# Attention products in float32, the two heads of a pair by turns, in four mixers of a three-block network

## The chip, the cores and the metric

One core of a Trainium2 chip runs the whole network as one program. The metric is the device time of one execution in microseconds; lower is better. All inputs and outputs are float32.

## The reference

The network takes 256 tokens of width 1024 through three blocks, with 16 heads of 64 (8 in the last mixer). Each mixer ends in the same sum: probabilities times values, head by head.

```python
def reference(x, ...):
    x = first_block(x, ...)    # FoX attention, then NSA attention, RMS norms
    x = second_block(x, ...)   # 8 stick-breaking + 8 dilated-window heads, then SwiGLU
    return third_block(x, ...) # pool mixer + MoBA attention (8 heads), then PEER experts

# fox_mixer, per block of 128 queries
logits = einsum('bhqd,bhkd->bhqk', q, k) * scale + c_q - c_k     # causal mask
p = softmax(logits)
outs.append(einsum('bhqk,bkhd->bqhd', p, v))
return (o * silu(z)) @ w_out

# nsa_mixer: 3 branches per head, gated
o = g0 * (p_c @ v_c) + g1 * (p_s @ v_s) + g2 * (p_w @ v_w)       # compressed, selected, window
return (o * silu(z)) @ w_out
```

With 256 tokens all selected blocks and windows cover the whole causal past, so each branch but the compressed one is 256 x 256 causal attention: a query block of 128 has 128 or 256 keys, three blocks of 128 x 128 in all.

## The kernel before, in words

Activations lie transposed, width on the 128 partitions and the 256 tokens along the free axis. A big projection (`proj`, `mm3`, lines 456 to 460) is done in F32R, a rounded float32 that TensorE streams faster: input and weight are each split into a high and a low part, and each tile takes three products, high x high, low x high, high x low. The weights come by DMA (SP's queue) as 128 x 1024 tiles, ScalarE makes the high part (line 241), VectorE the low part (line 242), some tiles ahead.

Inside a mixer the attention is woven between projections. `weave(main, (side, rate))` runs the generator of the projections, and after each step lets the side generator take some steps at the rate given (0.4 in fox, 4 in NSA, 0.55 in mixer2, 0.4 in mixer3). That sets the order in which the code is emitted; a scheduler then sets each engine's own order from it, which is fixed when the program is built. PE, ScalarE (ACT), VectorE (DVE) and GpSimd (POOL) each take their instructions in that order.

In each mixer a head pair is one 128-row tile (`c`): head 2c in rows 0 to 63, head 2c+1 in rows 64 to 127. For a head the scores are made (line 553), normalised to `pn` [128, 384] (line 586), transposed by PE in three 128 x 128 pieces (lines 592 to 594, or `transposed`, line 624), and copied from PSUM. The 384 columns are 256 queries for the first 128 keys and 128 queries for the second. Then come the AV products, of which there are two forms:

- Fox and mixer2 use F32R. `values` (lines 609 and 610) splits the values into `vh` and `vl` when the projection is read out of PSUM; `probs` (lines 618 and 619) splits the probabilities of a head pair into `pth` (ACT) and `ptl` (DVE); `pair_av` (line 636) makes 6 products for the pair, with the values of both heads as 128 stationary columns and the probabilities of both heads streaming, three of 512 columns and three of 256. Only one half of the result's rows is of use for each head, so `o` is [128, 2, 256], and `gated_pair` (line 654, fox) or `finish` (line 1131, mixer2) reads it in two halves. In mixer2's stick-breaking heads the probabilities come as `ptw` straight out of an exponential on ACT (line 1178), not by a transpose.
- NSA and mixer3 use float32. `attn_transpose` copies the transposed probabilities to `ptw` (line 596, DVE or ACT); `attn_av` makes two products for one head, 256 and 128 query columns (lines 603 and 604), with 64 stationary columns `vN`.

In NSA a side step makes two branches of two heads, and the compressed branch `comp` (lines 982 to 1001), a chain of one PE, eight DVE and one ACT instruction. Then `trans` transposes four probability tiles and, last, the compressed ones (line 1012), and `av` puts the compressed product (line 1021) and the four heads' products into one `o`. In mixer3 the AV product of a head comes two steps behind its scores.

The stretches of the trace are: fox 0 to 163 us (woven from 44 to 134), NSA 163 to 357 (206 to 331), mixer2 357 to 500 (375 to 476), SwiGLU to 703, mixer3 703 to 870 (735 to 820), PEER to the end.

Of the kernel before, what the change touches and what calls it, by code (L numbers as in the profile page):

```python
# [9 lines left out]
F32 = mybir.dt.float32  # L10
# [5 lines left out]
OP = mybir.AluOpType  # L16
# [254 lines left out]
def program(tc, A, out, upto=99):  # L271
    nc = tc.nc
    ctx = ExitStack()
    with ctx:
# [325 lines left out]

        def attn_av(o, pt, v, start=True, stop=True):

            nc.tensor.matmul(o, v(0), pt[:, 0:256], start=start, stop=False)
            nc.tensor.matmul(o[:, 128:256], v(1), pt[:, 256:384], start=False, stop=stop)

        def values(dst, c, p, r):

            hi, lo = (t[:, c[0], c[1]] for t in dst)
            nc.scalar.mul(hi, p, r)
            nc.vector.scalar_tensor_tensor(lo, p, r, hi.bitcast(F32), op0=OP.mult, op1=OP.subtract)  # L610

        def probs(pt, h, src):


            if h % 2 == 0:
                pt[h // 2] = [ph.tile([P, 2, 384], F32R, name=n, bufs=2) for n in ("pth", "ptl")]
            hi, lo = (t[:, h % 2, :] for t in pt[h // 2])
            nc.scalar.copy(hi, src)
            nc.vector.tensor_tensor(lo, src, hi.bitcast(F32), op=OP.subtract)

        def transposed(pn):
            p = ps.tile([P, 384], F32, name="t")
            for i in range(3):
                nc.tensor.transpose(p[:, i * P:i * P + P], pn[:, i * P:i * P + P], ident)
            return p

        def pair_av(pt, v, c):


            o = ps.tile([P, 2, S], F32, name="o")  # L630
            hi, lo = pt
            for kb in range(2):
                q = slice(0, S) if kb == 0 else slice(S, S + P)
                vh, vl = (t[:, kb, c] for t in v)
                for i, (w, x) in enumerate(((vh, hi), (vl, hi), (vh, lo))):
                    nc.tensor.matmul(o[:, :, kb * P:], w, x[:, :, q], start=kb == 0 and i == 0, stop=kb == 1 and i == 2)
            return o

# [7 lines left out]
        def gated(og, c, po, sz):  # L646
            t = wk.tile([P, S], F32, name="sp")
            nc.vector.tensor_tensor(t, po, sz[:, c, :], op=OP.mult)
            split(og, c, t)

        def gated_pair(og, c, o, sz):
            t = wk.tile([P, S], F32, name="sp")
            for e, a in enumerate(HALF):
                nc.vector.tensor_tensor(t[a], o[a, e, :], sz[a, c, :], op=OP.mult)
            split(og, c, t)
# [32 lines left out]
        def fox(st1):  # L688
# [50 lines left out]

            vN = [ph.tile([P, 2, D], F32R, name=n) for n in ("vh", "vl")]  # L740

            def v_evac(c, tb, p):
                if held:
                    f_evac(*held.pop())
                values(vN, (tb, slice(c * 512, c * 512 + 512)), p, rc[:, tb:tb + 1])

# [10 lines left out]
            def fox_attn():  # L757
                st, pt = {}, {}
                for i in range(NH + 3):
                    if i < NH:  # L760
                        h = i
                        while cnt["qk"] <= h // 2:
                            yield
                        pe, s = attn_scores((sel[:, h:h + 1].to_broadcast([P, P]), c3), C["causal"], stacks[h // 2], h % 2)
                        st[h] = attn_norm(pe, s)
                        yield
                    if 1 <= i <= NH:
                        probs(pt, i - 1, transposed(st[i - 1]))
                        yield
                    if i >= 3 and i % 2 == 1:  # L770
                        c = (i - 3) // 2
                        o = pair_av(pt.pop(c), vN, slice(c * P, c * P + P))
                        while cnt["z"] <= c:
                            yield
                        gated_pair(og, c, o, sz)
                        yield
# [17 lines left out]
        def nsa(st1):  # L794
# [159 lines left out]
            def attn():  # L954
# [48 lines left out]

                def trans(c):
                    for e in range(2):
                        for b in range(2):
                            stage[c, e, b] = attn_transpose(stage[c, e, b], CP[b])
                            yield
                    p = ps.tile([32, 256], F32, name="t")
                    c2 = stage[c, "c"]  # L1010
# [4 lines left out]
                    stage[c, "c"] = t  # L1015
                    yield

                def av(c):
                    gp = c // 4
                    o = ps.tile([P, S], F32, name="o")  # L1020
                    nc.tensor.matmul(o, VCB[:, gp, :], stage[c, "c"], start=True, stop=False)
                    for e in range(2):
                        oh = o[e * 64:e * 64 + 64, :]
                        g = 2 * gp + e
                        for b in range(2):
                            attn_av(oh, stage[c, e, b], lambda kb: vN[:, kb, b * 256 + g * 64:b * 256 + g * 64 + 64], False, b == 1)
                            yield
                    while cnt["z"] <= c:
                        yield
                    gated(og, c, o, sz)  # L1030
                    yield

                for i in range(9):
                    if i:
                        while len(done) < 2:
                            yield
                        yield from comp(i - 1)
                    if i < 8:
                        while cnt.get("nq", 0) <= i:
                            yield  # L1040
                        yield from scores(i)
                    if i:
                        yield from trans(i - 1)
                        yield from av(i - 1)

# [47 lines left out]
        def mixer2(st1):  # L1093
# [18 lines left out]

            vN = [ph.tile([P, 2, D], F32R, name=n) for n in ("vh", "vl")]

            def v_evac(c, tb, p):
                values(vN, (tb, slice(c * 512, c * 512 + 512)), p, rc[:, tb:tb + 1])

# [10 lines left out]
            def finish(c, po):  # L1128
                o = ph.tile([P, S], F32, name="fo", bufs=2)
                for e, a in enumerate(HALF):  # L1130
                    nc.scalar.copy(o[a], po[a, e, :])
                sq = wk.tile([P, S], F32, name="sq")
                nc.scalar.activation(sq, o, AF.Square)
                p = ps.tile([P, S], F32, name="t")
# [8 lines left out]
            def attn():  # L1143
                st, pt = {}, {}

                for i in range(19):
# [36 lines left out]
                    if i >= 3 and i % 2 == 1 and i <= 17:  # L1183
                        c = (i - 3) // 2
                        finish(c, pair_av(pt.pop(c), vN, slice(c * P, c * P + P)))
                        yield
# [73 lines left out]
        def mixer3(st1):  # L1260
# [58 lines left out]
            def attn():  # L1319
                st, po = {}, {}  # L1320
                for i in range(11):
# [8 lines left out]
                    if 1 <= i <= 8:  # L1330
                        st[i - 1] = attn_transpose(st[i - 1])
                        yield
                    if 2 <= i <= 9:
                        h = i - 2
                        c = h // 2
                        if h % 2 == 0:
                            po[c] = ps.tile([P, S], F32, name="o")
                        attn_av(po[c][(h % 2) * 64:(h % 2) * 64 + 64, :], st[h], lambda kb: vN[:, kb, h * 64:h * 64 + 64])
                        if h % 2 == 1:
                            nc.scalar.copy(oa[0][:, c, :], po[c])  # L1340
                            nc.vector.tensor_tensor(oa[1][:, c, :], po[c], oa[0][:, c, :].bitcast(F32), op=OP.subtract)
                        yield
# [415 lines left out]
```

## Time and profile before

| what | value |
|---|---|
| median of 3 runs | 1694.55 us (1691.9 to 1695.58) |
| the profiled execution | 1694.25 us |
| its span in the trace | 1692.4 us |
| mean granted TensorE clock | 0.994 |
| PE, DVE, ACT, POOL busy | 96%, 77%, 58%, 11% |
| woven part of fox, NSA, mixer2, mixer3 | 90, 125, 101, 85 us |

A row of the timeline gives the start, the duration, the engine, the line, the operation, its output and inputs, the sizes, and in brackets the idle time before it with the instruction that ended it. Matmuls overlap, so the price of one is the distance between two starts, not its duration. The mean durations of groups and the waits are sums over the window named.

### The profile page before, as it was taken

The page shows a single profiled execution, that of the slowest core. Times are in us where ns is not written, and L with a number is a line of the kernel's source. Part 1 is how long each engine was busy: PE and PEld are TensorE (multiplying, and loading weights), DVE is VectorE, ACT ScalarE, POOL GpSimd, SP SyncE. Part 2 cuts the span into 40 slices and gives each one's busy share as a digit, 9 for nine tenths or more (in the row PEclk, how much of TensorE's full clock was granted, in tenths as well). Part 3 has the DMA queues.
Part 4 walks back from the last instruction along what each step waited for, and adds up shares of the span by engine and source line. Part 5 has one row for each costly group of instructions (what it writes and reads, how often), then busy time and mean ns, then how long its engine had stood idle before and what let it go on. Part 6 is the DMA issues. An engine that isn't in the chain of part 4 may idle for free. (4 is left out here: it accounts for less than half of the span.)

```text
span 1692.4 us, 31723 instructions
## 1 busy us (share of the span) xinstructions
PE 1628.3 (96%) x12052; PEld 1500.7 (89%) x12052; DVE 1301.9 (77%) x2715; ACT 976.2 (58%) x1853; POOL 189.4 (11%) x198
## 2 busy tenths in 40 slices
PE   8999899989899999999999999999999999999997
PEld 7999888778789999889989899999999988888886
DVE  7888788689866776777668998889999656666665
ACT  6875567558855455566644555555544555555554
POOL 2000244340130000111037000000000000000000
PEclk9999999999999999999999999999999999999999
DMA  7445551277537787545545445555455556555563
GB/s 256 138 138 155 163 174 63 103 262 239 173 101 245 256 267 242 165 128 166 187 153 174 162 162 175 163 164 163 164 171 162 187 189 197 193 193 193 193 195 116
DMA packets 84088, 300.07 MB, mean 177 GB/s; under 512 B 10144, under 2 KB 11040, under 8 KB 83680
## 3 DMA queue, kind: packets, MB, share of 16 engines
q1 hardware_dynamic: 83360, 296.39, 53.4%
q8 instruction: 94, 1.54, 0.4%
q10 hardware_dynamic: 576, 1.66, 0.3%
q14 instruction: 58, 0.48, 0.1%
HBM read 296.04 MB, written 1.05 MB: 176 GB/s over the span
## 5 line engine op out<-in xcount | busy, mean ns | idle before, releaser
L242 DVE TENSOR_TENSOR wlo<-wraw,whi 128x1024 fp32r<-128x1024 f32 x486 | 600.6, 1239 | 160.5 <-ACT whi L241 158.0
L241 ACT CAST whi<-wraw 128x1024 fp32r<-128x1024 f32 x504 | 529.9, 1054 | 330.4 <-PE pj L459 104.1
L458 PE MATMUL pj<-hxh,whi 128*128 128x256 f32 x1448 | 411.9, 285 | 7.7 <-DVE vl L610 5.2
L460 PE MATMUL pj<-hxh,wlo 128*128 128x256 f32 x1448 | 405.1, 280 | 1.7 <-DVE wlo L242 1.1
L459 PE MATMUL pj<-hxl,whi 128*128 128x256 f32 x1448 | 405.5, 280 | 0.7 <-DVE hxl L1201 0.4
L458 PEld LDWEIGHTS pj<-hxh,whi 128*128 128x128 f32 x1448 | 273.7, 189 | 12.4 <-DVE vl L610 6.0
L460 PEld LDWEIGHTS pj<-hxh,wlo 128*128 128x128 f32 x1448 | 273.0, 189 | 3.6 <-DVE wlo L242 2.2
L459 PEld LDWEIGHTS pj<-hxl,whi 128*128 128x128 f32 x1448 | 273.2, 189 | 2.7 <-DVE hxl L1201 1.1
L1632 PE MATMUL s<-whi,hxl 128*128 128x512 f32 x512 | 157.7, 389 | 0.0
L1632 PE MATMUL t<-whi,hxl 128*128 128x512 f32 x512 | 157.6, 389 | 0.0
L1620 ACT CAST hxl<-a 128x256 fp32r<-128x256 f32 x128 | 51.9, 407 | 151.7 <-PE t L1632 150.0
L458 PE MATMUL s<-hxh,whi 128*128 128x256 f32 x456 | 129.1, 283 | 1.7 <-DVE st L580 1.7
L460 PE MATMUL s<-hxh,wlo 128*128 128x256 f32 x456 | 127.3, 279 | 1.3 <-DVE wlo L242 1.3
L459 PE MATMUL s<-hxl,whi 128*128 128x256 f32 x456 | 127.1, 279 | 0.1
L458 PE MATMUL t<-hxh,whi 128*128 128x256 f32 x432 | 121.8, 282 | 0.4 <-ACT whi L241 0.4
L460 PE MATMUL t<-hxh,wlo 128*128 128x256 f32 x432 | 119.9, 278 | 2.1 <-DVE wlo L242 2.1
L459 PE MATMUL t<-hxl,whi 128*128 128x256 f32 x432 | 119.7, 277 | 0.3 <-DVE hxl L379 0.3
L1632 PEld LDWEIGHTS t<-whi,hxl 128*128 128x128 f32 x512 | 96.1, 188 | 19.9
L1632 PEld LDWEIGHTS s<-whi,hxl 128*128 128x128 f32 x512 | 96.0, 188 | 20.0 <-ACT hxl L1620 0.2
L1621 DVE TENSOR_TENSOR hxl<-a,hxl 128x256 fp32r<-128x256 f32 x128 | 54.4, 425 | 62.2 <-PE t L1632 60.4
L299 DVE SCALAR_TENSOR_TENSOR wraw<-wraw,cb 128x1024 f32<-128x1024 f32 x48 | 58.9, 1227 | 45.7 <-DMA wraw<-in_ada 45.6
L458 PEld LDWEIGHTS s<-hxh,whi 128*128 128x128 f32 x456 | 86.3, 189 | 2.1 <-issue 2.0
(409 smaller groups left out, 3387.7 us busy)
## 6 DMA issues: line engine op xcount, KB each, us to landing
wraw<-in_pu SPq DMA_DIRECT2D x128, 512.0 KB
wraw<-in_pv SPq DMA_DIRECT2D x128, 512.0 KB
wraw<-in_b_ffn SPq DMA_DIRECT2D x66, 512.0 KB
wraw<-in_ada SPq DMA_DIRECT2D x48, 512.0 KB
wraw<-in_b_qk SPq DMA_DIRECT2D x24, 512.0 KB
wraw<-in_fox_qk SPq DMA_DIRECT2D x16, 512.0 KB
wraw<-in_b_o SPq DMA_DIRECT2D x16, 512.0 KB
wraw<-in_b_g SPq DMA_DIRECT2D x16, 512.0 KB
```

The costliest lines, as they stand in the source:

```text
L241: nc.scalar.copy(hi, r)
L242: (nc.gpsimd if self.np in self.on_pool else nc.vector).tensor_tensor(lo, r, hi.bitcast(F32), op=OP.subtract)
L299: nc.vector.scalar_tensor_tensor(t, t, 1.0, cb, op0=OP.mult, op1=OP.mult, accum_out=modT[:, i:i + 1])
L458: nc.tensor.matmul(o, wh, xh, start=start, stop=False)
L459: nc.tensor.matmul(o, wh, xl, start=False, stop=False)
L460: nc.tensor.matmul(o, wl, xh, start=False, stop=stop)
L1620: nc.scalar.copy(ah, src)
L1621: nc.vector.tensor_tensor(al, src, ah.bitcast(F32), op=OP.subtract)
L1632: nc.tensor.matmul(acc[tb][h], x[:, t], w[:, h * 512:h * 512 + 512], start=n == 0 and i == 0, stop=n == P - 1 and i == 2)
```

## The change

- Fox and mixer2 keep the values as one float32 tile `vN`, written by ACT alone, and the probabilities as `ptw`, by one copy on DVE (`attn_transpose`). `values`, `probs`, `transposed`, `pair_av` and `gated_pair` are gone. The stick-breaking heads use the exponential's output as it is.
- `attn_av` makes the four float32 products of a pair by turns: the first head's 256 columns into the upper half of `o`, the second head's into the lower half, then the first's 128, the second's 128.
- `o` is [128, 256], so fox gates it in one DVE instruction, and `finish` copies it in one on ACT and squares it straight from PSUM.
- NSA's `trans` and `av` become `trans_av`: first the compressed probabilities are transposed, then for each branch both heads' probabilities, the compressed product (first branch only), and `attn_av` for the pair. One head's copy is on DVE, the other's on ACT (before: one branch's on DVE, the other's on ACT).
- In mixer3 the products come per pair, two or three steps behind the scores.
- The small gap tiles between the pools are the same in both files, and so are the addresses of the weights and the PSUM tiles.

```diff
-        def attn_av(o, pt, v, start=True, stop=True):
-
-            nc.tensor.matmul(o, v(0), pt[:, 0:256], start=start, stop=False)
-            nc.tensor.matmul(o[:, 128:256], v(1), pt[:, 256:384], start=False, stop=stop)
-
-        def values(dst, c, p, r):
...
-        def probs(pt, h, src):
...
-        def transposed(pn):
...
-        def pair_av(pt, v, c):
...
+        def attn_av(o, pts, v, start=True, stop=True):
+
             for kb in range(2):
...
+                for e, a in enumerate(HALF):
+                    nc.tensor.matmul(o[a, kb * P:], v(e, kb), pts[e][:, kb * S:kb * P + S], start=start and not kb, stop=stop and kb == 1)
...
-            vN = [ph.tile([P, 2, D], F32R, name=n) for n in ("vh", "vl")]
+            vN = ph.tile([P, 2, D], F32, name="vN")
...
-                values(vN, (tb, slice(c * 512, c * 512 + 512)), p, rc[:, tb:tb + 1])
+                nc.scalar.mul(vN[:, tb, c * 512:c * 512 + 512], p, rc[:, tb:tb + 1])
...
                     if 1 <= i <= NH:
-                        probs(pt, i - 1, transposed(st[i - 1]))
+                        st[i - 1] = attn_transpose(st[i - 1])
                         yield
                     if i >= 3 and i % 2 == 1:
                         c = (i - 3) // 2
-                        o = pair_av(pt.pop(c), vN, slice(c * P, c * P + P))
+                        o = ps.tile([P, S], F32, name="o")
+                        attn_av(o, [st.pop(2 * c + e) for e in range(2)], lambda e, kb: vN[:, kb, c * P + e * 64:c * P + e * 64 + 64])
...
-                        gated_pair(og, c, o, sz)
+                        gated(og, c, o, sz)
...
-                def trans(c):
...
-                def av(c):
...
+                def trans_av(c):
+                    gp = c // 4
                     p = ps.tile([32, 256], F32, name="t")
...
                     nc.vector.tensor_copy(t, p)
...
+                    for b in range(2):
+                        pts = []
+                        for e in range(2):
+                            pts.append(attn_transpose(stage.pop((c, e, b)), CP[e]))
                             yield
+                        if not b:
+                            o = ps.tile([P, S], F32, name="o")
+                            nc.tensor.matmul(o, VCB[:, gp, :], t, start=True, stop=False)
+                        attn_av(o, pts, lambda e, kb: vN[:, kb, b * 256 + gp * P + e * 64:b * 256 + gp * P + e * 64 + 64], False, b == 1)
+                        yield
...
-                for e, a in enumerate(HALF):
-                    nc.scalar.copy(o[a], po[a, e, :])
+                nc.scalar.copy(o, po)
...
-                            probs(pt, h, w)
+                            st[h] = w
...
-                            probs(pt, h, transposed(st[h]))
+                            st[h] = attn_transpose(st[h])
...
-                    if 2 <= i <= 9:
...
+                    if i >= 3 and i % 2 == 1 and i <= 9:
+                        c = (i - 3) // 2
+                        o = ps.tile([P, S], F32, name="o")
+                        attn_av(o, [st.pop(2 * c + e) for e in range(2)], lambda e, kb: vN[:, kb, c * P + e * 64:c * P + e * 64 + 64])
```

The scheduler's order on PE moves with it. In fox, in the middle of the weave, one head pair stood so on PE before (`pj` is a projection; `pth`, `ptl` the two parts of the probabilities):

```order
L460 MATMUL pj<-hxh,wlo 128x256
L636 MATMUL o<-pth,vh 128x512
L636 MATMUL o<-pth,vl 128x512
L636 MATMUL o<-ptl,vh 128x512
L636 MATMUL o<-pth,vh 128x2x128
L636 MATMUL o<-pth,vl 128x2x128
L636 MATMUL o<-ptl,vh 128x2x128
L458 MATMUL pj<-hxh,whi 128x256
```

and stands so now:

```order
L458 MATMUL pj<-hxh,whi 128x256
L459 MATMUL pj<-hxl,whi 128x256
L460 MATMUL pj<-hxh,wlo 128x256
L605 MATMUL o<-ptw,vN 64x256 x2
L605 MATMUL o<-ptw,vN 64x128 x2
L458 MATMUL pj<-hxh,whi 128x256
```

The six products of 128 columns have become four of 64, with nothing between them here.

In NSA, in the middle of the weave, PE had before (`cm_...` are the compressed probabilities, `ct` their transpose):

```order
L1012 MATMUL t<-ident,cm_3474 32x128 x2
...
L1021 MATMUL o<-ct,VCB 128x256
L603 MATMUL o<-ptw,vN 64x256
L604 MATMUL o<-ptw,vN 64x128
L603 MATMUL o<-ptw,vN 64x256
L604 MATMUL o<-ptw,vN 64x128
L603 MATMUL o<-ptw,vN 64x256
L604 MATMUL o<-ptw,vN 64x128
L982 MATMUL t<-KC,qk 128x32 x2
```

and has now:

```order
L592 MATMUL t<-ident,pn 128x128
L593 MATMUL t<-ident,pn 128x128
L594 MATMUL t<-ident,pn 128x128
L983 MATMUL o<-ct,VCB 128x256
L605 MATMUL o<-ptw,vN 64x256
L592 MATMUL t<-ident,pn 128x128
L593 MATMUL t<-ident,pn 128x128
L594 MATMUL t<-ident,pn 128x128
L460 MATMUL pj<-hxh,wlo 128x256
L605 MATMUL o<-ptw,vN 64x256
L605 MATMUL o<-ptw,vN 64x128
L932 MATMUL s<-k_2489,q_3503 128x256
```

Three heads' products stood together before; now one product stands alone, then transposes and a projection, then two more, then scores, and the fourth comes behind them.

At the end of NSA's weave the last group had this order before:

```order
L592 MATMUL t<-ident,pn 128x128
L593 MATMUL t<-ident,pn 128x128
L594 MATMUL t<-ident,pn 128x128
L459 MATMUL pj<-hxl,whi 128x256
L460 MATMUL pj<-hxh,wlo 128x256
L459 MATMUL s<-hxl,whi 128x256
L460 MATMUL s<-hxh,wlo 128x256
L1012 MATMUL t<-ident,cm_4246 32x128 x2
L1021 MATMUL o<-ct,VCB 128x256
```

and has this now:

```order
L459 MATMUL s<-hxl,whi 128x256
L460 MATMUL s<-hxh,wlo 128x256
L972 MATMUL t<-ident,cm_4201 32x128 x2
L592 MATMUL t<-ident,pn 128x128
L593 MATMUL t<-ident,pn 128x128
L594 MATMUL t<-ident,pn 128x128
L592 MATMUL t<-ident,pn 128x128
L593 MATMUL t<-ident,pn 128x128
L594 MATMUL t<-ident,pn 128x128
```

The transpose of the compressed probabilities, which stood behind the head's transposes, stands in front of them.

Between two instructions that are not of this kind the products of a pair can be cut. In the changed order, A and B being the 256-column products of the first and second head, Ah and Bh the 128-column ones, and | a cut:

| mixer | pairs | in one block | A \| B Ah Bh | cut twice | others |
|---|---|---|---|---|---|
| fox | 8 | 6 | 1 | 0 | 1 A B Ah \| Bh |
| NSA | 16 | 8 | 6 | 2 | 0 |
| mixer2 | 8 | 5 | 1 | 0 | 2: one block with the next pair's A behind it, then that pair's B Ah Bh |
| mixer3 | 4 | 0 | 3 | 1 | 0 |

## Rows read from the trace of the kernel before

**Rows 1.** Page, section 1: busy us (share of the span) and number of instructions.

```profile
PE 1628.3 (96%) x12052; PEld 1500.7 (89%) x12052; DVE 1301.9 (77%) x2715; ACT 976.2 (58%) x1853; POOL 189.4 (11%) x198
```

**Rows 2.** Windows: stretch, its us, then each engine's busy us, granted clock, DMA share.

```profile
44.00:134.00 90.00, 86.21 (x694) 83.08 (x693) 80.16 (x210) 68.40 (x165) 4.11 (x4) 1.00 0.40 131
206.00:331.00 125.00, 116.28 (x878) 101.85 (x877) 98.63 (x334) 79.45 (x216) 53.62 (x73) 0.99 0.33 108
375.00:476.00 101.00, 91.22 (x643) 81.39 (x644) 82.39 (x170) 83.23 (x196) 11.22 (x20) 0.98 0.58 191
```

**Rows 3.** PE timeline in fox, one head pair in F32R.

```profile
59.19 0.39 PE L636 MATMUL o<-pth,vh 128*128 128x512 f32 x1
...
60.22 0.29 PE L458 MATMUL pj<-hxh,whi 128*128 128x256 f32 x1
```

**Rows 4.** PE timeline in mixer3, one head in float32.

```profile
779.03 0.28 PE L460 MATMUL pj<-hxh,wlo 128*128 128x256 f32 x1
779.24 0.65 PE L603 MATMUL o<-ptw,vN 128*64 128x256 f32 x2
...
780.26 0.29 PE L459 MATMUL pj<-hxl,whi 128*128 128x256 f32 x1
```

**Rows 5.** PE timeline in NSA, one head and then two by turns.

```profile
295.01 0.65 PE L603 MATMUL o<-ptw,vN 128*64 128x256 f32 x2
...
295.71 0.65 PE L603 MATMUL o<-ptw,vN 128*64 128x256 f32 x4
...
296.51 0.63 PE L982 MATMUL t<-KC,qk 128*128 128x32 f32 x4
```

**Rows 6.** PE timeline in mixer3, a first product that stands alone.

```profile
746.59 0.28 PE L460 MATMUL pj<-hxh,wlo 128*128 128x256 f32 x1
746.80 0.65 PE L603 MATMUL o<-ptw,vN 128*64 128x256 f32 x2
747.38 0.39 PE L553 MATMUL s<-stc,str 128*128 128x256 f32 x1
```

**Rows 7.** Timeline at the values of fox (first row) and of mixer2.

```profile
36.27 0.39 PE L458 MATMUL pj<-hxh,whi 128*128 128x256 f32 x1 [1.13 <-DVE vl L610]
...
376.21 1.26 ACT L609 ACTIVATE vh<-pj,rcol 128x512 fp32r<-128x512 f32 x2
377.48 1.40 DVE L610 SCALAR_TENSOR_TENSOR vl<-pj,rcol,vh 128x512 fp32r<-128x512 f32 x2
378.27 0.58 PE L458 MATMUL pj<-hxh,whi 128*128 128x256 f32 x1 [4.03 <-DVE vl L610]
```

**Rows 8.** Windows: the stretch behind mixer2's wait for the values.

```profile
378.00:381.60 3.60, 3.33 (x15) 3.33 (x16) 3.60 (x6) 1.04 (x1) 0.00 (x0) 0.53 0.78 255
```

**Rows 9.** Waits (us in total, times, longest): fox 44 to 134.5, then mixer2 375 to 476.

```profile
PE s L553 <- ACT stc L543: 1.7, 2, 1.3
...
PE s L553 <- ACT str L542: 1.3, 2, 0.8
...
ACT whi L241 <- DMA wraw<-in_b_qk: 10.8, 5, 3.4
...
PE t L624 <- POOL pn L586: 3.3, 3, 1.5
```

**Rows 10.** Groups by line (busy us, mean ns): fox 44 to 139, then mixer2 375 to 476.

```profile
L618 ACT CAST pth<-t 128x384 fp32r<-128x384 f32 x16 | 7.5, 467 | 0.7 <-PE t L624 0.7
...
L1131 ACT COPY fo<-o 64x256 f32<-64x256 f32 x16 | 5.9, 368 | 0.9 <-PE o L636 0.6
L619 DVE TENSOR_TENSOR ptl<-ptw,pth 128x384 fp32r<-128x384 f32 x8 | 4.4, 553 | 0.1
```

**Rows 11.** PE timeline at the end of NSA's weave, last group.

```profile
323.87 0.63 PE L982 MATMUL t<-KC,qk 128*128 128x32 f32 x4
...
327.71 0.38 PE L1012 MATMUL t<-ident,cm 128*32 128x128 f32 x2 [0.52 <-DVE cm L1000]
328.59 0.69 PE L1021 MATMUL o<-ct,VCB 32*128 32x256 f32 x2 [0.50 <-DVE ct L1014]
```

More of the change, by code (lines that the diff above doesn't have):

```diff
@@ L599, in program @@
         CP = (nc.vector.tensor_copy, nc.scalar.copy)
-        def attn_av(o, pt, v, start=True, stop=True):
-            nc.tensor.matmul(o, v(0), pt[:, 0:256], start=start, stop=False)
-            nc.tensor.matmul(o[:, 128:256], v(1), pt[:, 256:384], start=False, stop=stop)
-        def values(dst, c, p, r):
-            hi, lo = (t[:, c[0], c[1]] for t in dst)
-            nc.scalar.mul(hi, p, r)
-            nc.vector.scalar_tensor_tensor(lo, p, r, hi.bitcast(F32), op0=OP.mult, op1=OP.subtract)
-        def probs(pt, h, src):
[L615 to L619, printed above, removed]
-        def transposed(pn):
[L622 to L625, printed above, removed]
-        def pair_av(pt, v, c):
-            o = ps.tile([P, 2, S], F32, name="o")
-            hi, lo = pt
-            for kb in range(2):
[L633 to L637, printed above, removed]
+        def attn_av(o, pts, v, start=True, stop=True):
+            for kb in range(2):
+                for e, a in enumerate(HALF):
+                    nc.tensor.matmul(o[a, kb * P:], v(e, kb), pts[e][:, kb * S:kb * P + S], start=start and not kb, stop=stop and kb == 1)
         def resid(nxt):
@@ L648, in gated @@
             nc.vector.tensor_tensor(t, po, sz[:, c, :], op=OP.mult)
-            split(og, c, t)
-        def gated_pair(og, c, o, sz):
-            t = wk.tile([P, S], F32, name="sp")
-            for e, a in enumerate(HALF):
-                nc.vector.tensor_tensor(t[a], o[a, e, :], sz[a, c, :], op=OP.mult)
             split(og, c, t)
@@ L757, in fox_attn @@
             def fox_attn():
-                st, pt = {}, {}
+                st = {}
                 for i in range(NH + 3):
@@ L1002, in comp @@
                     yield
-                def trans(c):
[L1005 to L1008, printed above, removed]
+                def trans_av(c):
+                    gp = c // 4
                     p = ps.tile([32, 256], F32, name="t")
-                    c2 = stage[c, "c"]
+                    c2 = stage.pop((c, "c"))
                     for qb in range(2):
@@ L1014, in trans @@
                     nc.vector.tensor_copy(t, p)
-                    stage[c, "c"] = t
                     yield
-                def av(c):
[L1019 to L1026, printed above, removed]
-                            yield
+                    for b in range(2):
+                        pts = []
+                        for e in range(2):
+                            pts.append(attn_transpose(stage.pop((c, e, b)), CP[e]))
+                            yield
+                        if not b:
[3 more added lines that the diff above has]
+                        yield
                     while cnt["z"] <= c:
@@ L1042, in attn @@
                     if i:
-                        yield from trans(i - 1)
-                        yield from av(i - 1)
+                        yield from trans_av(i - 1)
             drain(proj(4, hx, c_evac, banks=("s", "t")))
@@ L1111, in mixer2 @@
                 nc.gpsimd.tensor_scalar(xT[:, kt, :], xT[:, kt, :], V["gf"][:, kt:kt + 1], ALPHA, op0=OP.mult, op1=OP.mult)
-            vN = [ph.tile([P, 2, D], F32R, name=n) for n in ("vh", "vl")]
+            vN = ph.tile([P, 2, D], F32, name="vN")
             def v_evac(c, tb, p):
-                values(vN, (tb, slice(c * 512, c * 512 + 512)), p, rc[:, tb:tb + 1])
+                nc.scalar.mul(vN[:, tb, c * 512:c * 512 + 512], p, rc[:, tb:tb + 1])
             def qk_evac(c0, p, m):
@@ L1129, in finish @@
                 o = ph.tile([P, S], F32, name="fo", bufs=2)
-                for e, a in enumerate(HALF):
-                    nc.scalar.copy(o[a], po[a, e, :])
+                nc.scalar.copy(o, po)
                 sq = wk.tile([P, S], F32, name="sq")
-                nc.scalar.activation(sq, o, AF.Square)
+                nc.scalar.activation(sq, po, AF.Square)
                 p = ps.tile([P, S], F32, name="t")
@@ L1143, in attn @@
             def attn():
-                st, pt = {}, {}
+                st = {}
                 for i in range(19):
@@ L1184, in attn @@
                         c = (i - 3) // 2
-                        finish(c, pair_av(pt.pop(c), vN, slice(c * P, c * P + P)))
+                        o = ps.tile([P, S], F32, name="o")
+                        attn_av(o, [st.pop(2 * c + e) for e in range(2)], lambda e, kb: vN[:, kb, c * P + e * 64:c * P + e * 64 + 64])
+                        finish(c, o)
                         yield
@@ L1319, in attn @@
             def attn():
-                st, po = {}, {}
+                st = {}
                 for i in range(11):
@@ L1332, in attn @@
                         yield
-                    if 2 <= i <= 9:
[L1334 to L1341, printed above, removed]
+                    if i >= 3 and i % 2 == 1 and i <= 9:
+                        c = (i - 3) // 2
+                        o = ps.tile([P, S], F32, name="o")
+                        attn_av(o, [st.pop(2 * c + e) for e in range(2)], lambda e, kb: vN[:, kb, c * P + e * 64:c * P + e * 64 + 64])
+                        nc.scalar.copy(oa[0][:, c, :], o)
+                        nc.vector.tensor_tensor(oa[1][:, c, :], o, oa[0][:, c, :].bitcast(F32), op=OP.subtract)
                         yield
```

## The prediction

> **What bounds the kernel now.** The page's first section comes first: TensorE (PE) is busy in 96% of the span, VectorE (DVE) in 77%, ScalarE (ACT) in 58% [rows 1]. So time is won or lost where PE streams longer or shorter, or stops. The windows of three stages that the change touches show how much stopping there is: PE is busy 86.21 of 90 us in the fox weave, 116.28 of 125 in NSA's, 91.22 of 101 in mixer2's, with the granted clock at or near 1.00 [rows 2]. After that I read the PE timeline around the products of the probabilities with the values (the AV products), for the price of each form [rows 3 to 6], and the waits for what stops PE [rows 7 to 10].
>
> The sum is made against the profiled execution, 1694.25 us, a span of 1692.4 and 1.85 around it; the median of the runs shown is 0.3 higher. About 0.2%, 3.4 us, is what a measurement of this kernel can tell from no change.
>
> **Price of the old and the new form.** One pair of heads in fox or mixer2 is now six F32R products, 59.19 to 60.22: 1.03 us, with neighbours that keep their usual distance of 0.117 [rows 3]. One head in float32 with 64 columns of values (mixer3) is two products; from the projection before it (779.03) to the second projection behind it (780.26) are 1.23 us, less two usual distances of 0.117: 1.00 us [rows 4]. Of this some 0.65 is streaming; the other 0.35 is the edge of a block, a slower start in and a slower restart out of it.
>
> What two heads cost side by side, no row of fox, mixer2 or mixer3 shows, since each head stands by itself there. NSA's rows do: one head takes 0.70 us (295.01 to 295.71), then two heads whose products alternate in the two halves of the columns take 0.80 (295.71 to 296.51) [rows 5]. So the second head costs about 0.1 beside the first. A pair in the new form, uncut, is then an estimated 1.00 + 0.06 to 0.10, and I take 1.06, near the 1.03 of before.
>
> The Trainium skill, "TensorE: Matmul & The Clock Gate", Part 3 (Packing small matmuls), under "What overlaps and what doesn't", says otherwise: weight loads pass a matmul in flight only where the row group differs, and matmuls start and end strictly in order. Both heads here use all 128 rows, so by it the second head would pay its full stream. The row of 0.80 speaks against that; it is rival C.
>
> But the order in which the scheduler puts the four products matters: where a projection or a score stands between them, the edge is paid again. A lone first product costs 0.78 us: 0.21 + 0.58 between starts, less 0.117, and 0.1 for the slow restart [rows 6]. So a pair cut after its first product is 0.78 + 1.06 = 1.84; cut twice 2.19, an edge of 0.35 more; one whose last product alone is cut off 1.57, some 0.5 more than uncut, of which 0.35 is edge. A fifth product put behind an uncut pair I take at 0.37, without an edge. These are estimates from rows 4 to 6.
>
> **Term 1, PE time of the AV products.** Counted in the order of the changed program:
> - Fox: 6 uncut, one of 1.84, one of 1.57: 9.77 us, against 8 x 1.03 = 8.24. +1.5.
> - Mixer2: 5 uncut, one pair fused with the next one's first product (1.43 + 1.06), one of 1.84: 9.63 against 8.24. +1.4.
> - NSA: 16 pairs, 8 uncut, 6 of 1.84, 2 of 2.19: 23.9. Before, each of 8 groups of four head-branches took an estimated 2.36 in one block (0.70 + 0.80 + 0.70 by rows 5, and 0.16 for its start) or 2.71 in two, an edge more (4 of each): 20.3. +3.6.
> - Mixer3: 3 pairs of 1.84, one of 2.19: 7.7. Before, 6 heads of 1.00 and 2 that were cut, an edge more, 1.35: 8.7. −1.0.
>
> Together +5.5. Bounds: +2 if the cut blocks cost less at their edges than the lone product of rows 6 (its follower is a score matmul), +8 if fused ones cost what cut ones do.
>
> **Term 2, evacuation of the values.** Now ACT makes the high part, DVE the low part, and the next projection waits for the latter: 1.13 us at 36.27, 4.03 at 378.27 [rows 7]. Afterwards ACT alone reads the accumulator. In fox a DVE step of some 0.7 (two take 1.40 in mixer2) and its handover go: −1.0. In mixer2 ACT's two copies start at 376.21, so the first ends at about 376.9; DVE's stood behind another split until 377.48, its first ended at about 378.2 [rows 7]: −1.3. The rest of the 4.03 stays, as it is ACT that is late next. Sum −2.3.
>
> **Term 3, clock.** Right behind that stop the granted clock is 0.53 for 3.6 us, the lower level, 1.2 GHz, after 4.0 us without PE work [rows 8]. A stop of 2.7 us remains, so I leave the slow stretch as it is: 0, bound −1.7, half of it.
>
> **Term 4, fox.** PE stops 1.7 + 1.3 us for ACT's score operands [rows 9]. ACT loses 16 copies of 0.467 = 7.5 us [rows 10] of 68.40 [rows 2]; DVE's 16 subtractions become 16 copies of the same 384 columns, taken as equal. Eleven per cent less ACT should take half of the stops: −1.5, bounds 0 (another engine or the order is late instead) and −3.0.
>
> **Term 5, mixer2.** PE is idle 101 − 91.22 = 9.8, about 3.3 of which is the wait of term 2 inside the window; 6.5 remain, such as 3.3 for the normalised probabilities of POOL [rows 9]. ACT loses 16 copies at fox's 0.467, and 8 x 0.368 where two half copies become one [rows 10]: 10.4 of 83.23. DVE loses 8 x 0.553 = 4.4 [rows 10] of 82.39; for the other eight heads a copy replaces a subtraction. Two engines at 82% lose 12% and 5%, so I take −4.0 of the 6.5; bounds 0 and −6.5. What is late next is POOL, which does not change, and the weights: ACT already waits 10.8 us for their transfers in this window [rows 9], and a faster stage asks for them earlier. SP's issues and POOL's work stay the same in number.
>
> **Term 6, NSA's waits.** The transposed compressed probabilities come before everything else of the head pair in the new order, where they came last. From the score product (323.87) to its use (327.71) are 3.84 us with little else running on DVE [rows 11]. In the new order some 41 to 46 PE instructions (4.8 to 5.4 us at 0.117) stand between them in most groups, which covers it; but for the last two groups only 18 to 20 (2.1 to 2.3 us), so there about 1.5 us each is uncovered. Of today's tail, two stops of 0.5 disappear, and the transposes' copies now stop PE with no projections left behind them. +1.5, bounds −4 and +4, half a microsecond, the size of those two stops [rows 11], won or lost in each of 8 groups.
>
> **Sum.** +5.5 − 2.3 + 0 − 1.5 − 4.0 + 1.5 = −0.8, so 1694.25 − 0.8 = 1693.4 us: no change that could be measured. The terms' own bounds carry this case from about 1689 to 1697.5.
>
> **Rivals.**
> A, the stops vanish. ACT's relief is what holds PE in fox and mixer2, so all of terms 4 and 5 comes back (−3.0, −6.5), the short stop at 378 no longer lowers the clock (−1.7), and the NSA order costs nothing beyond its products: 5.5 − 2.3 − 3.0 − 6.5 − 1.7 = −8.0: 1686.2. For it: ACT is the busiest helper in mixer2 (83.23 of 101) [rows 2]. Against: most of mixer2's stops name POOL [rows 9].
>
> B, the NSA order becomes a wait, slower. DVE is busy 98.63 of 125 us in that weave [rows 2], so the 3.84 us chain, measured in its quiet tail, is longer in the middle; PE takes its instructions in order, and everything behind the transposed probabilities waits. It decides as soon as the chain exceeds the 4.8 to 5.4 us in front of it; one extra stop of half a microsecond in each of 8 groups is +4. With the stops elsewhere unchanged: 5.5 − 2.3 + 4 = +7.2, so 1701.4.
>
> C, the two heads' products do not run side by side. Then each of the 36 pairs pays the second head's 0.65 where I took 0.06: 36 x 0.59 = +21, about 1714.5. Against it stands the 0.80 of rows 5.
>
> That the change does nothing of what it says is excluded: the product rows themselves are others.
>
> **How the numbers follow.** Forecast 50%, A 25%, B 20%, C 5%. Forecast's own spread puts 12 of its 50 points below 1691, 36 within 0.2%, 2 above. Faster by over 0.2%: 25 + 12 = 37%; within 0.2%: 36%; slower: 20 + 5 + 2 = 27%. The range reaches from 1.7 beyond A (the other half of the slow stretch) to B, 1684.5 to 1701.5, and leaves out C, the outer half of B and little of A; the forecast's own is 1689 to 1697.5.
>
> **What would show it.** Right: in fox and mixer2 the uncut pair takes 1.0 to 1.1 us between the projections around it, the second head starting within 10 ns of the first; PE's wait at the values shrinks to 2.7 in mixer2 and nearly none in fox; PE busy in NSA's weave rises by 3 to 4 us; the three windows of rows 2 end within a few microseconds of before. Wrong: PE stops over 1 us at the transposed probabilities in most NSA groups (B), pairs of 1.6 us or more without a cut (C), mixer2's weave shorter by over 8 us (A).

## The result and the profile after

The changed kernel takes 1682.36 us (median of 5 runs, 1678.82 to 1683.96) against 1695.58 for the kernel before (5 runs): ratio 0.9918, 95% interval 0.9897 to 0.9939, so 10 to 17 us less. A second sample gave 0.9912 (0.9888 to 0.9936). I had forecast 1693.4 within 1684.5 to 1701.5; the time lies below the range. The profiled execution is 1683.96 us with a span of 1682.1.

The page's first section, as in [rows 1]:

```profile
PE 1626.9 (97%) x12084; PEld 1491.6 (89%) x12084; DVE 1293.5 (77%) x2691; ACT 963.3 (57%) x1813; POOL 185.7 (11%) x198
```

PE's busy time fell by 1.4 us, the span by 10.3. So what went is mostly time in which PE stood still. To see where, I measured stages by progress: the 7536 projection matmuls are the same work in the same order of code in every kernel, so the distance between two of them, by number, is a stage's length. Windows cut so, of the kernel before (fox, NSA's weave, mixer2 from the first projections of its values to its end, mixer3's weave; columns as in [rows 2]):

```profile
40.47:163.56 123.09, 119.22 (x964) 114.94 (x963) 105.90 (x255) 87.55 (x198) 7.46 (x10) 1.00 0.44 142
201.21:332.93 131.72, 123.00 (x935) 108.28 (x933) 103.14 (x339) 82.99 (x221) 54.97 (x77) 0.99 0.33 108
345.96:484.67 138.71, 125.96 (x837) 110.53 (x835) 116.25 (x220) 100.72 (x223) 31.53 (x35) 0.99 0.59 196
736.39:816.28 79.89, 77.53 (x608) 71.98 (x607) 60.10 (x123) 54.77 (x113) 7.62 (x10) 1.00 0.46 143
```

and of the changed kernel:

```profile
40.45:161.92 121.47, 119.59 (x980) 112.44 (x979) 102.99 (x247) 82.00 (x182) 7.39 (x10) 1.00 0.43 145
198.00:326.78 128.78, 123.25 (x934) 104.27 (x932) 104.14 (x339) 84.46 (x221) 52.31 (x77) 1.00 0.34 111
339.83:473.65 133.82, 124.13 (x853) 107.95 (x851) 111.79 (x208) 91.80 (x198) 31.60 (x35) 0.99 0.62 203
726.90:805.91 79.01, 77.15 (x608) 71.46 (x607) 59.53 (x123) 54.98 (x113) 7.51 (x10) 1.00 0.44 149
```

Fox is 1.6 us shorter, NSA's weave 2.9, mixer2 4.9, mixer3 0.9. The first number behind the comma is PE's busy time: in NSA it rose by 0.25 while idle time (length less busy) fell from 8.72 to 5.53. Stages without a change of code are no still ground: the SwiGLU part differs from that of the kernel before by −3.5 to +2.0 us over the profiles of this study, the stretch before NSA's weave by −2.7 to +0.7, and mixer2 itself, in the five profiles that leave it as it was, by −1.4 to +0.6. NSA's weave is stiller, −0.6 to +0.4 where its code is the old one. That is why single profiles are read by stage here.

An uncut pair in fox, after, which answers to [rows 3]:

```profile
73.96 0.28 PE L460 MATMUL pj<-hxh,wlo 128*128 128x256 f32 x1
74.17 0.87 PE L605 MATMUL o<-ptw,vN 128*64 128x256 f32 x8
74.97 0.38 PE L458 MATMUL pj<-hxh,whi 128*128 128x256 f32 x1
75.19 0.28 PE L459 MATMUL pj<-hxl,whi 128*128 128x256 f32 x1
```

From 73.96 to 75.19 are 1.23 us; less two distances of 0.117, 1.00 for two heads, what one head alone cost in [rows 4].

### The profile page after: what moved, and what is told of

Its sections match the earlier page's. It is cut to its first block, busy times and chain, and to the rows that moved or that the text cites. A ratio compares the mean times of both kernels' runs of the same rounds, so it can differ in the third digit from the quotient of the medians.

```text
span 1682.1 us, 31714 instructions
## 1 busy us (share of the span) xinstructions
PE 1626.9 (97%) x12084; PEld 1491.6 (89%) x12084; DVE 1293.5 (77%) x2691; ACT 963.3 (57%) x1813; POOL 185.7 (11%) x198
## 5 line engine op out<-in xcount | busy, mean ns | idle before, releaser
L460 PEld LDWEIGHTS s<-hxh,wlo 128*128 128x128 f32 x456 | 85.8, 188 | 1.6 <-DVE wlo L242 1.6
```

The source lines that it names most:

```text
L460: nc.tensor.matmul(o, wl, xh, start=False, stop=stop)
```

## The experiments

Fifteen runs follow, one of them the changed kernel again. "Before" and "changed" name the two kernels of the result; ratios are to runs of the kernel before on the same chip.

**Each mixer alone.** Each of four kernels takes one mixer's code from the changed kernel and the rest from before; instruction orders outside that mixer stay as they were. The edit is that mixer's part of the diff ahead; mixer3's, for one:

```diff
-                    if 2 <= i <= 9:
...
+                    if i >= 3 and i % 2 == 1 and i <= 9:
...
+                        attn_av2(o, [st.pop(2 * c + e) for e in range(2)], ...
```

> Only fox is changed. Theory (each mixer's own gain adds up, as the two traces divide it): fox is 1.6 us shorter, the rest as before, so about 1.6 us below the kernel before. My prediction had -1.0. Rival (the gain is chance of clock stretches elsewhere): no difference, or one that stands outside fox in the trace.

> Only NSA is changed. Theory: about -3 to -4.5 us, with the weave 3 us shorter, half of it the slow-clock stretch at 316.7 that is gone because the wait before it is gone. The prediction had +5.1 us here. Rival: the trace's gain here was a chance of that run's clock; then +1 to +5 us.

> Only mixer2 is changed. Theory: -5 us, of it 1.3 at the evacuation of the values and 3.6 in the weave and the first projections behind it. The prediction had -3.9. Rival: below 1 us, when the stops of POOL and of the weights' transfers come back as others.

> Only mixer3 is changed. Theory: -0.9 us, all of it fewer edges of AV blocks on PE. The prediction had -1.0. Rival: none that can be told apart at this size; the trace's stage length decides.

| changed alone | median us | ratio (95%) | its own stage |
|---|---|---|---|
| fox | 1690.18 | 0.9971 (0.9958 to 0.9984) | −1.5, and −1.0 ahead of it |
| NSA | 1692.39 | 0.9981 (0.9971 to 0.9991) | −2.9 |
| mixer2 | 1685.45 | 0.9949 (0.9934 to 0.9964) | −6.2 |
| mixer3 | 1693.11 | 0.9986 (0.9975 to 0.9996) | −0.9 |

All four are faster, and the stages repeat what the two first traces show, but for mixer2 (−6.2 for −4.9). The −1.0 is the evacuation of fox's values; in the changed kernel's profile a start that was 1.0 later hides it. So the gain is no chance, and NSA, where I had +5.1, gives −2.9. By the totals the four add up to some 19 us where the changed kernel has 14; the intervals allow both, so it is the stages that divide the gain, and they add up to 12.5.

**By turns or head after head.**

```diff
-            for kb in range(2):
-                for e, a in enumerate(HALF):
+            for e, a in enumerate(HALF):
+                for kb in range(2):
```

> The changed kernel with the four products of a pair head after head (first head 256, 128 columns, then the second head) in place of by turns. Theory (the second head's products run beside the first's whatever their order, as in the rows of 0.80 us, which were written head after head): an uncut pair still takes 0.8 to 0.9 us between its first start and its end, total within 1 us of the changed kernel's 1682. Rival (only by turns do they run side by side): an uncut pair takes 1.3 us or more, about +0.5 for each of some 21 uncut pairs and less for the cut ones, +8 to +15 us in all, slower than or like the kernel before.

1684.66 us, ratio 0.9937 (0.9921 to 0.9954). The pair at the same place in fox:

```profile
73.68 0.28 PE L460 MATMUL pj<-hxh,wlo 128*128 128x256 f32 x1
73.89 0.88 PE L605 MATMUL o<-ptw,vN 128*64 128x256 f32 x8
74.70 0.39 PE L458 MATMUL pj<-hxh,whi 128*128 128x256 f32 x1
```

0.81 from the block's start to the projection, as by turns (0.80). In the trace the second head's first product starts 13 ns after the first head's, though the first head's other product stands between them in the order. The turns are not what makes the heads run side by side. NSA's weave is 3.6 us longer than in the changed kernel: PE stands still for 1.9 us more, and from 313.8 to 320.6 the granted clock is 0.5, which is worth up to 3.4. The total is 2 to 4 us longer by medians and ratios, and the intervals overlap; that it lies within 1 us, as I expected, is not shown.

**The place of the compressed probabilities.** Three kernels. First, the changed kernel with them transposed late:

```diff
                 def trans_av(c):
-                    p = ps.tile([32, 256], F32, name="t")
...
                     for b in range(2):
...
                         if not b:
+                            p = ps.tile([32, 256], F32, name="t")
...
```

> The changed kernel, but the compressed probabilities of NSA are transposed after the first branch's two heads, just before their product, as late as the pairing lets them. My prediction (placing them first costs a wait of about 1.5 us in each of the last two groups): NSA's weave 1.5 to 3 us shorter. Theory now (the trace shows only 0.7 us of such waits): no difference beyond 1 us, or longer, since the order around it was good by its spacing.

1686.48 us, 0.9954 (0.9938 to 0.9970). NSA's weave is 133.51 us, 4.7 longer than in the changed kernel; PE's idle time in it is 9.16 us in place of 5.53, and a stretch at the lower clock, at 245.8, is worth 1.7. PE's waits there in the changed kernel:

```profile
PE t L972 <- DVE cm L963: 0.7, 2, 0.4
```

and in this one:

```profile
PE t L978 <- DVE cm L963: 4.0, 3, 1.7
```

The later the consumer stands, the later its input. From the start of the compressed score product to the end of their finished probabilities the eight groups take 7.3 us on average before, 5.2 in the changed kernel, 7.5 here. Second, the reverse, the kernel before with this block moved from last to first in `trans`:

```diff
                 def trans(c):
-                    for e in range(2):
-                        for b in range(2):
...
                     p = ps.tile([32, 256], F32, name="t")
...
+                    for e in range(2):
+                        for b in range(2):
...
```

> The kernel before with one block moved: in NSA's step the compressed probabilities are transposed first instead of last; nothing else is changed. Theory (the place of the consumer sets how early the scheduler puts the chain's DVE instructions): the chain from the compressed scores to its end takes 5 to 6 us on average where it took 7.3, PE waits for it less, the weave is 2 to 5 us shorter. My prediction's term: +1.5 us. Rival (the gain came from pairing and spacing): within 1 us of before.

1699.30 us, 1.0018 (1.0002 to 1.0034): slower, the expectation failed in the sum. Its NSA window:

```profile
202.50:340.28 137.78, 130.99 (x935) 110.16 (x933) 101.17 (x339) 83.84 (x221) 53.52 (x78) 0.98 0.32 103
```

The chain did shrink, to 5.3 us, and idle time fell from 8.72 to 6.79. But the AV products now lie in 23 blocks in place of 12 and cost 29.0 us where they cost 19.3, and a second stretch at the lower clock adds 1.7. So the early place does shorten the chain, and alone it does not pay in the old step. Third, the old step with the products by pairs and turns:

```diff
-                    for e in range(2):
...
-                        for b in range(2):
-                            attn_av(oh, stage[c, e, b], ...
+                    for b in range(2):
+                        attn_av2(o, [stage[c, e, b] for e in range(2)], ...
```

> The kernel before, with NSA's products alone by pairs and turns; the transposes, the compressed probabilities and the steps stay in the old order. Theory (NSA's gain comes from the new order of transposes and products, which leaves PE fewer stops): the weave is within 1 us of before and keeps its slow-clock stretch. Rival (the pairing itself gives it): the weave is 3 us shorter, as where NSA alone was changed.

1698.96 us, 1.0029 (1.0016 to 1.0041). The weave is as before (131.96), so pairing alone gives NSA nothing. In its profile the 13 us behind the weave are 6 us longer: 3.1 of that is a wait for a weight, and 1.7 the lower clock behind it; why the weight was late is open.

**Filling the wait for mixer2's values.**

```diff
             drain(proj_nat(2, hx, v_evac, ("s", "pj")))
+            f = ps.tile([P, 512], F32, name="o")
+            for _ in range(16):
+                nc.tensor.matmul(f, hx[0][:, 7, 0:P], hx[0][:, 0:2, :], start=True, stop=True)
```

> The kernel before, with 16 matmuls added on PE where it waits for mixer2's values; they go to a PSUM tile that nothing reads. 16 x 0.216 = 3.5 us of the 4.0 to 4.4 us wait is filled. Theory (the low clock of 4 us follows PE's stop): the wait row shrinks to under 1 us, the granted clock stays 1.00 there, -1.7 us. Rival (the clock falls for other reasons, or the fillers push the projections back): the low clock stays at this place, or +0 to +1 us.

1695.40 us, 1.0003 (0.9991 to 1.0014).

```profile
374.39 3.84 PE L1191 MATMUL o<-hxh 128*128 128x512 f32 x16
378.87 0.39 PE L458 MATMUL pj<-hxh,whi 128*128 128x256 f32 x1 [0.64 <-DVE vl L610]
391.52 0.36 PE L553 MATMUL s<-stc,str 128*128 128x256 f32 x1 [3.98 <-ACT str L542]
```

The low clock behind the values is gone, as expected: it follows the stop. But PE stops at 391.5 instead, for ACT's score operands, and the window 392 to 396 has the lower clock (0.60). The stop that was filled moved to the next late input, and the 1.7 us that I expected did not come.

**Giving back mixer2's parts, one by one, in the changed kernel.** ACT's work (a copy of each head's probabilities that nothing reads), then the low part of the values, the second copy on the way to the products, and the old reading of the result:

```diff
+                        nc.scalar.copy(ph.tile([P, 384], F32R, name="pth", bufs=2), st[h])
```

> The changed kernel with 16 copies of the probabilities (128 x 384, about 0.5 us each, 8 us) given back to ACT in mixer2's weave; they go to a tile that nothing reads, so no product waits for them. Theory (mixer2's weave is shorter because ACT, at 82% there before, lost such work): mixer2 from its values to the end of its weave is 2 to 4 us longer than the 132.4 to 133.8 us of the changed kernel, though still under the 138.7 of before. Rival (it is shorter for the order, or for the products that no longer wait for a high and a low part): under 1 us longer.

```diff
+                nc.vector.scalar_tensor_tensor(vl[:, tb, c * 512:c * 512 + 512], p, rc[:, tb:tb + 1], hi, op0=OP.mult, op1=OP.subtract)
```

> The changed kernel with one thing of before given back in mixer2: DVE makes the low part of the values from the accumulator too, into a tile that nothing reads. My prediction's term 2: the projections behind it wait for DVE again, +1.3 us at the entry (from the last projection of NSA's out-part to the first scores), the rest of mixer2 as in the changed kernel. Rival (the wait there is for the weights' transfers anyway): within 1 us at the entry.

```diff
+                            nc.scalar.copy(y, w)
+                            st[h] = wk.tile([P, 384], F32, name="ptw")
+                            nc.vector.tensor_copy(st[h], y)
```

> The changed kernel with the probabilities of mixer2 passed through two copies again, ACT and then DVE, as the high and the low part were, and the product waits for the second. Theory (mixer2's second half of the gain comes at its last two head pairs, where no projections are left to hide the shorter way from probabilities to products): 2 to 4 us longer, from the last 20 us of the weave on. Rival (it comes from the single copy and the square straight from PSUM behind the products): under 1 us longer.

```diff
-                nc.scalar.copy(o, po)
+                for a in HALF:
+                    nc.scalar.copy(o[a], po[a, :])
...
-                nc.scalar.activation(sq, po, AF.Square)
+                nc.scalar.activation(sq, o, AF.Square)
```

> The changed kernel with mixer2's result read as before: two half copies on ACT, then the square from the copy. Theory of the run above: under 1 us longer. Rival: 1 to 3 us longer at the last two pairs, since the head's norm waits 0.6 to 0.8 us longer for each.

| given back | median us | ratio (95%) | mixer2, against before |
|---|---|---|---|
| nothing (two profiles) | 1682.36, 1681.15 | 0.9918, 0.9912 | −4.9, −6.3 |
| 8 us of ACT copies | 1678.89 | 0.9899 (0.9883 to 0.9914) | −6.2 |
| low part of the values | 1682.67 | 0.9915 (0.9898 to 0.9931) | −4.2 |
| second copy | 1682.77 | 0.9922 (0.9906 to 0.9939) | −4.4 |
| reading by halves | 1678.38 | 0.9897 (0.9880 to 0.9913) | −6.4 |

The ACT work costs nothing. For the other three the table alone does not do, since one stretch at the lower clock more or less, 1.7 us, is as large as what is looked for: the first profile of the changed kernel has one in mixer2, the repeat, the run with the ACT copies and the one with the reading by halves have none, the one with the second copy has one, the one with the low part has two. The low part brings the wait back,

```profile
371.94 0.46 PE L458 MATMUL pj<-hxh,whi 128*128 128x256 f32 x1 [4.26 <-DVE vl L1076]
```

and with it 1.9 to 2.6 us at the entry, against the profiles of the new mixer2 without the lower clock there; 1.7 of that is the lower clock right behind the stop. What the second copy costs is not shown: its mixer2 is 1.9 us longer than in the repeat, but 1.7 of that is the stretch at the lower clock, at 427.3, in the middle of the weave. Over the last two pairs it gains 1.2 us less than the repeat (1.9 for 3.1); before that stretch it was ahead of it. The reading costs nothing.

In progress, mixer2's gain is 2.5 to 3.5 us at its entry in those profiles (1.2 in the first one of the changed kernel), stays level through the weave, and rises by 3 over the last two pairs. Of these 3 the second copy takes back 1.2 in its one profile; the rest is open.

**Fewer cuts.** The head whose probabilities are copied last goes first:

```diff
             for kb in range(2):
-                for e, a in enumerate(HALF):
+                for e, a in ((1, HALF[1]), (0, HALF[0])):
```

> The changed kernel with the second head of a pair first in each turn. Its probabilities are copied last, so when its product can start the other's can too, and the order on PE then has 4 pairs with a cut where the changed kernel had 15. Theory (a cut costs about 0.8 us of PE, 1.77 against 1.00): AV blocks and edges some 8 us less in all, of which PE's stops take part back: -3 to -8 us against the changed kernel's 1682, most of it in NSA. Rival (the cut's lone product filled time in which PE would have waited for the second head's copy): within 2 us of 1682.

> The changed kernel once more, for a second sample beside the others of this chip. 1682 us, 12 to 14 us below the kernel before; the stages fox, NSA's weave, mixer2 and mixer3 repeat their -1.6, -2.9, -4.9, -0.9 within 1 us each, while the stretch before NSA's weave and the SwiGLU part move by up to 3 us either way with no change of code.

The repeat took 1681.15 us; its stages are −0.8 in fox, −2.9 in NSA, −6.3 in mixer2 and −0.9 in mixer3, so mixer2 misses the 1 us that I expected it to keep within. The reversed order took 1673.55 (1670.47 to 1675.52), ratio 0.9863 (0.9836 to 0.9889): the fastest kernel of the study. Its windows of NSA and mixer3:

```profile
200.03:324.75 124.72, 118.14 (x934) 102.22 (x932) 102.19 (x339) 84.14 (x221) 54.58 (x77) 1.00 0.35 114
...
719.38:795.93 76.55, 74.08 (x608) 70.22 (x607) 59.40 (x123) 54.83 (x113) 8.48 (x10) 1.00 0.47 152
```

The blocks of AV products go from 54 to 40, and their cost from 49.4 to 38.9 us. NSA's weave is 4.1 us shorter than in the changed kernel, with PE busy 5.1 less; mixer3's 2.5 shorter. A cut is paid on PE. Of the 10.5 us, 7.6 to 8.8 reached the total (against the repeat and against the first runs), much as the theory expected; PE's idle time in the four windows rose by 1.2.

## Why the prediction was wrong

| term | predicted | measured |
|---|---|---|
| 1, AV products, fox | 8.24 to 9.77 | 9.16 to 9.57 |
| 1, mixer2 | 8.24 to 9.63 | 9.46 to 9.21 |
| 1, NSA | 20.3 to 23.9 | 19.3 to 23.0 |
| 1, mixer3 | 8.7 to 7.7 | 8.9 to 7.6 |
| 2, values | −1.0, −1.3 | −1.0, −1.9 to −2.6 (1.7 of the latter the clock) |
| 3, low clock | 0 | −1.7 in NSA; 0 or −1.7 in mixer2, by profile |
| 4, fox's stops | −1.5 | −2.0 |
| 6, NSA's waits | +1.5 | −3.2 of idle time, −4.9 with all the rest |

(AV cost is the time inside a block plus what the distances into and out of it exceed the usual ones.)

The forecast was −0.8, the two profiles differ by −10.3. Of the 9.5 us between them, NSA's weave alone makes 8.0: +5.1 forecast, −2.9 measured.

**Term 6 failed, and with its sign.** It took the chain from the compressed scores as fixed, 3.84 us from [rows 11], and asked only whether enough PE work stands in front of the consumer. The chain is eight DVE instructions in an order that the scheduler makes: where their consumer comes early in the code, they come early on DVE. In the last group it took 2.98 us to its use, not 3.84, and in the last two groups, where I had 1.5 us of waiting each, PE waited 0.14 and 0.0 for it; it did so for 0.37 in two of the middle ones. NSA's −2.9 is +3.7 for its products, −1.7 for the clock, and so −4.9 for all the rest. Of that rest 3.2 is idle time of PE that went; the other 1.7 is busy time outside the products, and where it went was not followed up. Nor is the chain the larger part of the idle time. Two of PE's waits in NSA's weave before:

```profile
PE t L592 <- POOL pn L586: 1.9, 3, 1.4
PE t L1012 <- DVE cm L1000: 1.8, 2, 1.3
```

The second, for the chain, became the 0.7 shown above. The first, for probabilities that POOL normalises, is gone altogether in the changed kernel, and term 6 had put it at nothing; why POOL is no longer late was not tested. That the place of the consumer sets the chain's length is shown in both directions (7.3 to 5.2 to 7.5, and 5.3); that it does not pay alone is shown by the kernel at 1699. Which part of the new step keeps the cuts down beside it was not separated.

**Term 3 was part of it.** I looked at the low clock in mixer2 and left it. The other stretch, at 316.7 behind a stop of 1.75 us,

```profile
316.70:320.20 3.50, 3.47 (x16) 3.39 (x17) 2.37 (x6) 2.62 (x8) 2.65 (x5) 0.51 0.15 27
```

is gone: the eight profiles with the new NSA step (one of them with the heads' order reversed) have none in that weave, the five with the old step untouched have one each, worth 1.7 us. The new step does not exclude it: with the products head after head, and with the late transposition, one is there again. In mixer2 I left it at 0 because a stop of 2.7 us would remain. There all seven profiles with the old code have a stretch or more, and five of the ten with the new code have none.

**Term 1 was right in kind and missed 2.9 us in size,** +2.6 in place of +5.5. I counted the cuts of the new form and not those of the old one: 8 x 1.03 for fox and mixer2, where two of the eight old pairs in each were cut too. An uncut pair measured 1.00, not 1.06. NSA's +3.6 and mixer3's −1.0 held (+3.7, −1.3). PE's busy time in NSA's weave was to rise by 3 to 4 us and rose by 0.25, or 2.0 without the clock's 1.7: what the products cost more was in part saved beside them.

**Terms 2 and 4** were near in size. In mixer2 the wait at the values shrank further than I had it, from 4.03 to 1.31 us where 2.7 should remain, but the next stop, of 2.38, came at the first scores. **Term 5** had the size (−4.0 and +1.4; with term 2, −3.9 for mixer2, against −4.9 and −6.3) and the wrong reason: the weave's middle gained nothing, and the ACT work could be given back for nothing. The gain lies at the values and at the last two pairs.

**The rivals.** A, faster, came nearest in time (1686.2), but not by its mechanism in mixer2, for the same reason. B, a wait at the transposed probabilities, measured 0.7 us in all. C is excluded: two heads take 0.80, by turns or not. The Trainium skill, "TensorE: Matmul & The Clock Gate", Part 3 (Packing small matmuls), says under "What overlaps and what doesn't" that matmuls start in order; the start at 13 ns, ahead of a product that precedes it, disagrees for products in different column halves. The same part of the Trainium skill lists, under "Measured speedup vs the span model", matmuls packed by columns that run 2.38 times as fast, three at a time; the prediction passed over that when it took the Trainium skill as speaking for C.

## What to carry to other kernels

Where a scheduler sets the order, the length of a dependent chain is no constant to read from the trace: moving its consumer moves the chain, so read the chain in several groups, and count the edges of split products in the old order as carefully as in the new. When a pair of products may run side by side, put first the one whose input comes last: the other is ready by then, and less is put between them (54 blocks became 40 here). A stop that vanishes is worth something only if the next input is not late too, which a few filler products at the stop show in one run.

## What was unexpected in the hardware

Two float32 products of 64 columns in different halves run side by side also when they do not follow each other in the order (0.81 against 0.80 us per pair). A stretch at the lower clock is worth 1.7 us here (twice that for the long one at 313.8), and the number of such stretches differs between profiles of the same code: the changed kernel has one in mixer2 in its first profile (after a stop of 2.4 us at 380) and none there in the repeat, which is about the difference of −4.9 and −6.3.
